# A fp32 decoder layer on one core: input blocks at the start, state-space chunks and the merge of the attention groups respread over the schedule

## The chip, the cores and the metric

The kernel runs on 1 core of one Trainium2 chip. The metric is the device time of one execution in microseconds (us): 888.43 us, the median of 3 runs (888.11 to 888.56). Engines are named as in the profile: PE (TensorE), DVE (VectorE), ACT (ScalarE), POOL (GpSimd) and SP (SyncE, which issues most DMAs here).

## What is computed

One layer, S = 512 tokens, D = 1024, all in fp32:

```python
proj = x @ w_in            # q, k, v (3 dilation groups x 8 heads x 64), u (512), gate logits (2 x 1024)
outs, lses = attention(q, k, v)          # per group: out and log of the softmax denominator
attn = sum(softmax(lses, over groups) * outs)
y_attn = attn @ w_attn_br
states = scan(a_bar, b_bar * u)          # 32 groups of 16 channels, complex 64-dim states
y = gelu(Re(C states) + D u)
a, b = split(y @ w_glu); y_ssm = (a * sigmoid(b)) @ w_ssm_br
h = layer_norm(ALPHA * x + (gates[0] * y_attn + gates[1] * y_ssm) @ w_out)
out = layer_norm(ALPHA * h + (silu(h @ w_ff_gate) * (h @ w_ff_up)) @ w_ff_down)
```

In the kernel dilation group 0 is attention "kind 0", groups 1 and 2 are taken together as "kind 1"; the merge weighs kind 0 against kind 1 by their maxima and denominators.

## The kernel before

**Products.** Each fp32 operand is split into a high part (rounded, by ACT, L178) and a low part (the rest, by DVE, L179); `mm3` (L184) makes hi·hi, lo·hi and hi·lo, the lines L185, L186, L187 of the profile. A product with 8 blocks of 128 rows is 24 matmuls of 128x512.

**Weights.** They come as 1 MB units (two weight tiles each) by a DMA of SP into one of two raw buffers. `Weights.split` (ACT `whi`, DVE `wlo`) fills one of three slots; `release` at the end of a step frees a slot, and so lets the tile three steps later be split. A weight tile's `wlo` therefore stands in DVE's queue behind whatever a step gave to DVE before its end.

**Steps.** PE runs through steps n: 0 to 3 make u (the state-space input), 4 to 7 v of group 0 (each with a transposition `tv` one step later), 8 to 19 gates, 20 to 27 k and q of group 0, 28 to 51 v, k, q of groups 1 and 2, 52 to 55 gates. Then 4 GLU tiles (56 to 59), 8 branch tiles BR0 to BR7 (60 to 67; 0 to 3 read the GLU's `gh`, `gl`, 4 to 7 the merged attention `ath`, `atl`), the output product, the feed-forward part. All other work is hung into the steps by `at_step(n, fn)`: at n it runs in the middle of the step's tile (or behind it, in the GLU tiles), at n + 0.5 at its end. Small DVE operations of the state-space model wait in a list `late`, from which `drip(first, last, cols)` takes about `cols` columns every half step.

**What the change touches.** At the start x comes in five DMAs and the first u unit in three, in turn (L249 to L263); the first two u tiles are made together (`u_first`), the other two as steps 2 and 3. `u_turn` sends u through DRAM, `make_pm` (step 6) transposes the matrices `zs`, `state_inputs` (steps 8 and 8.5) makes 64 small matmuls each, in banks that the transpositions use too (scores: banks 3, 4; turned: 5, 6), and ACT copies the four banks out. `ssm_out` (24.5, 25.5) makes y and its GELU on ACT and DVE in turn. At the end `split_y` (55) splits y for the GLU, `merge_stats` (56) turns the statistics of both kinds into 8 rows (`stb`, `sts`), then come `merge_weights` (57, with a reciprocal), `merge_split` (58, hi and lo rows in `whl`) and four `merge_pair` (59.5 to 62.5), in which two matmuls for each kind, one for the hi rows and one for the lo rows, spread the weights over 128 partitions (`wb`), and DVE makes the merged output.

Of the kernel before, what the change touches and what calls it, by code (L numbers as in the profile page):

```python
# [1329 lines left out]
```

## Time and profile before

| | before |
|---|---|
| time, median of 3 runs | 888.43 us (888.11 to 888.56) |
| the profiled execution | 889.8 us, of it a span of 887.9 us |
| mean granted clock of PE over the span | 0.993 |
| busy: PE, DVE, ACT | 868.0, 496.0, 292.9 us |

The span is what the profiler records from the first to the last instruction; 1.9 us of the profiled execution lie outside it. Times of the trace are us from the span's start. PE's matmuls are pipelined: the record of a 128x512 matmul is 0.39 us long, and the next one starts 0.227 us after it, so the step from one start to the next is the cost of one. A wait is the idle time in brackets behind a row of the timeline, with the work that ended it.

### The profile page before, as it was taken

The numbers are of one execution on the slowest core, as the hardware profiler recorded it, in microseconds if no ns is written. First come the engines' busy times: TensorE is split into PE (matmuls) and PEld (weight loads), VectorE is DVE, ScalarE is ACT, GpSimd is POOL, SyncE is SP. The second block draws the span as 40 slices with busy tenths as digits, with TensorE's granted clock in tenths as the row PEclk, the third lists the DMA queues.
The fourth block names the chain that finished last, engine by engine and source line by source line (L and its number), as shares of the span: only waits on it lengthen the run. The fifth ranks groups of instructions, "written<-read, shape, count | busy, mean of one in ns | idle before, by whom it ended". The sixth has DMA issues, their size and how long they took to land.

```text
span 887.9 us, 11787 instructions
## 1 busy us (share of the span) xinstructions
PE 868.0 (98%) x4822; PEld 716.7 (81%) x4822; DVE 496.0 (56%) x951; ACT 292.9 (33%) x478; POOL 25.1 (3%) x26
## 2 busy tenths in 40 slices
PE   8989999989999999998999999999999999999996
PEld 5878888878878888876788898888888888888885
DVE  7865999765365455347876764444444444222237
ACT  5354332344442234554234233222222222211111
POOL 0000000000000000000000410000000000000004
PEclk9999999999999999999999999999999999999998
DMA  8832423234212212112316313222222222422203
GB/s 307 184 101 97 102 71 102 89 96 143 89 54 96 85 59 96 48 50 75 108 55 245 134 55 137 94 95 95 96 94 96 95 95 94 142 95 95 94 1 96
DMA packets 23782, 90.04 MB, mean 101 GB/s; under 512 B 5672, under 2 KB 10792, under 8 KB 14512
## 3 DMA queue, kind: packets, MB, share of 16 engines
q1 hardware_dynamic: 22144, 86.80, 29.4%
q10 hardware_dynamic: 1584, 2.48, 0.8%
q8 instruction: 38, 0.62, 0.3%
q14 instruction: 16, 0.13, 0.0%
HBM read 84.85 MB, written 4.42 MB: 101 GB/s over the span
## 4 chain that ended last, share of the span: by engine, by line
PE 48%; issue 40%; DVE 7%; ACT 3%; POOL 2%; DMA 1%; SPq 0%; DVEq 0%; POOLq 0%
PE pg L185 3%; PE pg L187 3%; PE pg L186 3%; PE pv L186 3%; PE pv L187 3%; PE pv L185 3%; PE pk L185 3%; PE pk L187 2%; PE pk L186 2%; PE pq L185 2%; PE pq L187 2%; PE pq L186 2%; PE s L764 2%; PE t L788 2%; PE o L802 2%
## 5 line engine op out<-in xcount | busy, mean ns | idle before, releaser
L179 DVE TENSOR_TENSOR wlo<-raw,whi 128x1024 fp32r<-128x1024 f32 x136 | 166.3, 1227 | 205.5 <-ACT whi L178 205.4
L178 ACT CAST whi<-raw 128x1024 fp32r<-128x1024 f32 x136 | 141.6, 1046 | 205.6 <-PE dn L187 74.8
L185 PE MATMUL fg<-hh,whi 128*128 128x512 f32 (+1 forms) x384 | 143.5, 374 | 0.0
L187 PE MATMUL fg<-hh,wlo 128*128 128x512 f32 (+1 forms) x384 | 143.4, 373 | 0.0
L186 PE MATMUL fg<-hl,whi 128*128 128x512 f32 (+1 forms) x384 | 143.4, 373 | 0.0
L186 PEld LDWEIGHTS fg<-hl,whi 128*128 128x128 f32 x384 | 72.3, 188 | 13.3
L187 PEld LDWEIGHTS fg<-hh,wlo 128*128 128x128 f32 x384 | 72.3, 188 | 13.3
L185 PEld LDWEIGHTS fg<-hh,whi 128*128 128x128 f32 x384 | 72.3, 188 | 13.3
L185 PE MATMUL dn<-whi,ff 128*128 128x512 f32 x168 | 66.0, 393 | 0.0
L187 PE MATMUL dn<-whi,ff 128*128 128x512 f32 x168 | 65.9, 392 | 0.0
L186 PE MATMUL dn<-wlo,ff 128*128 128x512 f32 x168 | 65.8, 392 | 0.0
L185 PE MATMUL pg<-x_hi,whi 128*128 128x512 f32 x128 | 51.0, 399 | 0.0
L187 PE MATMUL pg<-x_hi,wlo 128*128 128x512 f32 x128 | 50.5, 395 | 0.0
L186 PE MATMUL pg<-x_lo,whi 128*128 128x512 f32 x128 | 50.5, 395 | 0.0
L181 ACT ACTIVATE ff<-fth 128x512 fp32r<-128x512 f32 x22 | 13.9, 634 | 101.6 <-DVE fth L301 101.6
L301 DVE TENSOR_TENSOR fth<-fth,fg 128x512 f32<-128x512 f32 x22 | 15.1, 688 | 55.8 <-PE fg L187 55.6
L776 ACT ACTIVATE pt<-pt,st 128x256 f32<-128x256 f32 (+1 forms) x64 | 30.9, 485 | 45.7 <-DVE st L774 45.7
L186 PE MATMUL pv<-wlo,x_hi 128*128 128x256 f32 x128 | 37.0, 289 | 2.7 <-DVE wlo L179 2.7
L185 PE MATMUL pq<-x_hi,whi 128*128 128x512 f32 x96 | 38.2, 398 | 0.0
L185 PE MATMUL pk<-x_hi,whi 128*128 128x512 f32 x96 | 37.8, 394 | 0.0
L186 PE MATMUL pq<-x_lo,whi 128*128 128x512 f32 x96 | 37.5, 390 | 0.0
L187 PE MATMUL pq<-x_hi,wlo 128*128 128x512 f32 x96 | 37.4, 390 | 0.0
(247 smaller groups left out, 1566.0 us busy)
## 6 DMA issues: line engine op xcount, KB each, us to landing
raw<-in_w_in SPq DMA_DIRECT2D x27, 1024.0 KB, 4.8
raw<-in_w_gu SPq DMA_DIRECT2D x22, 1024.0 KB, 4.8
raw<-in_w_dn SPq DMA_DIRECT2D x11, 1024.0 KB, 4.7
raw<-in_w_br SPq DMA_DIRECT2D x4, 1024.0 KB, 4.8
raw<-in_w_out SPq DMA_DIRECT2D x4, 1024.0 KB, 4.7
raw<-in_w_glu SPq DMA_DIRECT2D x2, 1024.0 KB, 4.8
xn<-in_x SPq DMA_DIRECT2D x2, 1024.0 KB, 8.2
out_dram<-hn SPq DMA_DIRECT2D x13, 128.0 KB, 2.4
```

The lines of the kernel that those rows point to most:

```text
L178: act.copy(hi, src)
L179: dve.tensor_tensor(lo, src, hi.bitcast(F32), op=ALU.subtract)
L181: act.mul(hi, src, scale)
L185: pe.matmul(dst, a[0], b[0], start=first, stop=False)
L186: pe.matmul(dst, a[0], b[1], start=False, stop=False)
L187: pe.matmul(dst, a[1], b[0], start=False, stop=last)
L301: eng.tensor_tensor(o, a, b, op=op)
L764: pe.matmul(banks[hh][:, 256 * j + 128 * c : 256 * j + 128 * (c + nk)], z[0][rows, hp, qs], z[1][rows, hp, 128 * k0 : 128 * (k0 + nk)], st ...
L776: act.activation(pt[:, :n], pt[:, :n], AF.Exp, bias=mneg, scale=-1.0, accum_out=zsum)
L788: pe.transpose(tb[:, hh, cs], pts[hh][:, cs], ident)
L802: pe.matmul(ob[64 * hh : 64 * hh + 64, 128 * blk : 128 * blk + 128], z[2][:, kb, 64 * h : 64 * h + 64], tv[:, hh, 128 * c : 128 * c + 128] ...
```

## The change

- **Start.** Both u units come in blocks of x's rows: x block 0, u block 0, x block 1, u block 1 and so on (256 KB each up to block 3, then pairs of 512 KB). `u_tiles` makes all four u tiles at once, in banks 3 to 6: for each block four hi·hi, four with x's low part, four with the weights' low part. The first split waits for no `late` operations ahead of it.
- **State inputs.** `state_inputs` goes in four parts, at 7, 7.5, 8 and 8.5, of 32 matmuls and two copies each.
- **Drips and the state-space output.** `late` is taken by 2000 columns (4 to 9), 1600 (9 to 20) and 500 (20 to 28) for 1900 (4 to 20) and 700 (20 to 24.5). `ssm_out` moves to 28 and 29 with its GELU in batches of two halves, `turn_y` to 30, the attention turns of kind 0 from 27 + 1.5 j to 30 + 1.5 j.
- **Merge.** The statistics of kind 0 are turned at step 52; everything from `split_y` to the reciprocal stands at 55.5, `merge_split` at 57, the pairs at 58 to 61. Hi and lo rows stand in one operand of 40 rows (8 hi, 24 zero, 8 lo), so that `wb` is one matmul for each kind; POOL clears the operand.
- **Loops.** In the GLU loop what hangs on n comes after the tile's weights are released; a branch tile runs its first three blocks for both columns, then block 3 of the first, what hangs on n, and block 3 of the second.

```diff
-TURNS = [[27 + 1.5 * j for j in range(10)], ...
+TURNS = [[30 + 1.5 * j for j in range(10)], ...
-    load_x(0, 1)
-    load_u(slice(0, 2))
-    load_x(1, 2)
-    load_u(slice(2, 4))
-    load_x(2, 4)
-    load_u(slice(4, 8))
-    load_x(4, 6)
-    load_x(6, 8)
-    w.n_dma = 1
-    w.n_split = 2
+    for k0, k1 in ((0, 1), (1, 2), (2, 3), (3, 4), (4, 6), (6, 8)):
+        load_x(k0, k1)
+        load_u(k0, k1)
+    w.n_dma = 2
+    w.n_split = 4
...
-    late.take(14)
-    split_x(0)
-    late.take(6)
-    split_u(slice(0, 2))
...
+    for k in range(KT):
         split_x(k)
+        split(wup[0][k // 4][:, k % 4], wup[1][k // 4][:, k % 4], wu[k // 4][:, k % 4])
+        late.take(4 if k < 2 else 10)
...
+    def u_tiles():
+        bs = [bank(3 + e, f"pu{e}") for e in range(4)]
         for k in range(KT):
+            xk = kslice(xp, k)
+            for a, b in ((0, 0), (0, 1), (1, 0)):
+                for e in range(4):
+                    wk = kslice(wup, k, slice(128 * e, 128 * e + 128))
+                    pe.matmul(bs[e], wk[a], xk[b], start=(k + a + b == 0), stop=(k == KT - 1 and a == 1))
+        for e in range(4):
             u_evac(bs[e], e)
...
-    def state_inputs(r):
+    def state_inputs(r, m):
...
-        for m in range(2):
-            bs = [(scores, turned)[m](f"sb{r}{m}{half}") for half in range(2)]
+        bs = [(scores, turned)[m](f"sb{r}{m}{half}") for half in range(2)]
...
-            act.square(y2, yf)
-            ts(y2, y2, 0.044715, ALU.mult, 1.0, ALU.add)
-            tt(y2, y2, yf, ALU.mult)
-            act.activation(y2, y2, AF.Tanh, scale=math.sqrt(2.0 / math.pi))
-            stt(yf, y2, 1.0, yf, ALU.add, ALU.mult)
+        for a, b in zip(y2, yf):
+            act.square(a, b)
+            ts(a, a, 0.044715, ALU.mult, 1.0, ALU.add)
+            tt(a, a, b, ALU.mult)
+        for a, b in zip(y2, yf):
+            act.activation(a, a, AF.Tanh, scale=math.sqrt(2.0 / math.pi))
+            stt(b, a, 1.0, b, ALU.add, ALU.mult)
...
     def merge_split():
...
+        act.copy(sel, rope[64:104, 0].rearrange("h (p m) -> h p m", p=NPAIR))
+        pool.memset(hl[0:40, 0:1024].bitcast(F32), 0.0)
+        for (m, _), w_ in zip(merged["s"], merged["w"]):
+            tt(m, m, merged["z"], ALU.mult)
+            act.copy(w_[0:8], m)
+            tt(w_[32:40], m, w_[0:8].bitcast(F32), ALU.subtract)
...
-            for e in range(2):
-                pe.matmul(wb[kind], merged["sel"][:, hp, :], merged["w"][kind][e], start=(e == 0), stop=(e == 1))
+            pe.matmul(wb[kind], merged["sel"][:, hp, :], merged["w"][kind], start=True, stop=True)
...
-    drip(4, 20, 1900)
-    drip(20, 24.5, 700)
+    drip(4, 9, 2000)
+    drip(9, 20, 1600)
+    drip(20, 28, 500)
...
-    at_step(8, state_inputs, 0)
-    at_step(8.5, state_inputs, 1)
+    for r in range(2):
+        for m in range(2):
+            at_step(7 + r + 0.5 * m, state_inputs, r, m)
...
-        at_step(24.5 + rnd, ssm_out, rnd)
-    at_step(26.5, turn_y)
+        at_step(28 + rnd, ssm_out, rnd)
+    at_step(30, turn_y)
...
-    at_step(55, split_y)
-    at_step(56, merge_stats)
-    at_step(57, merge_weights)
-    at_step(58, merge_split)
+    at_step(52, merge_stats, 0)
+    for fn in (split_y, lambda: merge_stats(1), merge_shift, merge_sum, merge_reciprocal):
+        at_step(55.5, fn)
+    at_step(57, merge_split)
     for hp in range(NPAIR):
-        at_step(59.5 + hp, merge_pair, hp)
+        at_step(58 + hp, merge_pair, hp)
...
-        run_fill(N_GLU + n)
         th = at.tile([P, 512], F32, tag="sw", name=f"th{n}")
...
         w.release()
+        run_fill(N_GLU + n)
...
+        part(0, range(3))
+        part(1, range(3))
+        part(0, (3,))
+        run_fill(N_BR + n)
+        part(1, (3,))
```

**Three places in the order of instructions.** First DVE around the first `ssm_out`; `ysb` is y, `y2` its GELU, the `rope` rows belong to a q tile, `wlo` is a weight tile's low part. Before:

```order
L298 SCALAR_TENSOR_TENSOR ysb_1512<-y2_00_1569,ysb_1512 128x512
L301 TENSOR_TENSOR ysb_1512<-ysb_1512,yc00_1515 128x2x128
L301 TENSOR_TENSOR ysb_1512<-ysb_1512,yc01_1516 128x2x128
L295 TENSOR_SCALAR y2_01_1579<-y2_01_1579 128x512
L301 TENSOR_TENSOR y2_01_1579<-y2_01_1579,ysb_1512 128x512
L298 SCALAR_TENSOR_TENSOR ysb_1512<-y2_01_1579,ysb_1512 128x512
L714 STREAM_SHUFFLE swq01_1610<-pq01_1585 128x512
L301 TENSOR_TENSOR cqq01_1611<-pq01_1585,rope_105 128x512
L301 TENSOR_TENSOR swq01_1610<-swq01_1610,rope_105 128x512
L301 TENSOR_TENSOR q0_1474<-cqq01_1611,swq01_1610 128x4x128
L179 TENSOR_TENSOR wlo1_28_1617<-raw14_1437,whi1_28_1616 128x1024
```

and now:

```order
L297 TENSOR_TENSOR q0_1473<-cqq03_1609,swq03_1608 128x4x128
L179 TENSOR_TENSOR wlo2_30_1615<-raw15_1509,whi2_30_1614 128x1024
L297 TENSOR_TENSOR ysb_1644<-ysb_1644,yc00_1647 128x2x128
L297 TENSOR_TENSOR ysb_1644<-ysb_1644,yc01_1648 128x2x128
L297 TENSOR_TENSOR ysb_1644<-ysb_1644,yc00_1647 128x2x128
L297 TENSOR_TENSOR ysb_1644<-ysb_1644,yc01_1648 128x2x128
L291 TENSOR_SCALAR y2_00_1697<-y2_00_1697 128x512
L297 TENSOR_TENSOR y2_00_1697<-y2_00_1697,ysb_1644 128x512
L291 TENSOR_SCALAR y2_01_1698<-y2_01_1698 128x512
L297 TENSOR_TENSOR y2_01_1698<-y2_01_1698,ysb_1644 128x512
L294 SCALAR_TENSOR_TENSOR ysb_1644<-y2_00_1697,ysb_1644 128x512
L294 SCALAR_TENSOR_TENSOR ysb_1644<-y2_01_1698,ysb_1644 128x512
```

Before, the ten operations of the first `ssm_out` (the last six are shown) stand between two q tiles and ahead of the low part of the tile of step 28, `wlo1_28`. Now they stand behind `wlo2_30`, in steps 28 and 29, which have no rope; the ten of the second follow them directly, and then `wlo0_31`, the tile of step 31.

Second ACT from step 7 to step 9; `sb` are the banks of the state inputs, `sst` what they are copied into, `tv` the transposed v, `vt` v before it, `whi` a weight tile. Before:

```order
L733 COPY v0_436<-tv02_626 128x4x128
L726 COPY vt3_644<-pv03_606 128x4x128
L178 CAST whi1_10_646<-raw5_472 128x1024
L593 COPY sst0_680<-sb000_681 128x4x16x8
L593 COPY sst0_680<-sb001_682 128x4x16x8
L593 COPY sst0_680<-sb010_701 128x4x16x8
L593 COPY sst0_680<-sb011_702 128x4x16x8
L733 COPY v0_436<-tv03_721 128x4x128
L877 ACTIVATE gt0_658<-pg0_659,bgate_107 128x512
L178 CAST whi2_11_740<-raw5_472 128x1024
L593 COPY sst1_748<-sb100_749 128x4x16x8
L593 COPY sst1_748<-sb101_750 128x4x16x8
```

and now:

```order
L178 CAST whi2_9_594<-raw4_270 128x1024
L574 COPY sst0_628<-sb000_629 128x4x16x8
L574 COPY sst0_628<-sb001_630 128x4x16x8
L716 COPY v0_435<-tv02_649 128x4x128
L709 COPY vt3_667<-pv03_607 128x4x128
L178 CAST whi0_10_669<-raw5_471 128x1024
L574 COPY sst0_628<-sb010_682 128x4x16x8
L574 COPY sst0_628<-sb011_683 128x4x16x8
L574 COPY sst1_722<-sb100_723 128x4x16x8
L574 COPY sst1_722<-sb101_724 128x4x16x8
L716 COPY v0_435<-tv03_743 128x4x128
L864 ACTIVATE gt0_702<-pg0_703,bgate_116 128x512
```

The copies `sst` come in pairs, one pair ahead of the copy of `tv02` and two ahead of that of `tv03`, where all four of the first state input stood ahead of `tv03`.

Third DVE in the merge, from the sum of the denominators on; `sts` and `rope` hold the rows of both kinds, `th` and `gl` belong to the GLU tiles, `wlo` is a weight tile, `whl` the operand of the spreading matmuls. Before:

```order
L301 TENSOR_TENSOR zg_3710<-sts_3633 8x512
L840 RECIPROCAL zg_3710<-zg_3710 8x512
L298 SCALAR_TENSOR_TENSOR th1_3715<-th1_3715,gl10_3684 128x512
L182 SCALAR_TENSOR_TENSOR gl_3604<-th1_3715,gh_3603 128x512
L179 TENSOR_TENSOR wlo0_60_3721<-raw30_3494,whi0_60_3720 128x1024
L846 CAST selr_3750<-sel_3631 8x512
L301 TENSOR_TENSOR sts_3633<-sts_3633,zg_3710 8x512 x2
L301 TENSOR_TENSOR whl_3752<-sts_3633,whl_3752 8x512 x2
L298 SCALAR_TENSOR_TENSOR th2_3761<-th2_3761,gl20_3724 128x512
L182 SCALAR_TENSOR_TENSOR gl_3604<-th2_3761,gh_3603 128x512
L179 TENSOR_TENSOR wlo1_61_3767<-raw30_3494,whi1_61_3766 128x1024
```

and now:

```order
L297 TENSOR_TENSOR sts_3615<-rope_114,sts_3615 8x512
L831 RECIPROCAL sts_3615<-sts_3615 8x512
L294 SCALAR_TENSOR_TENSOR th0_3665<-th0_3665,gl00_3639 128x512
L182 SCALAR_TENSOR_TENSOR gl_3638<-th0_3665,gh_3637 128x512
L179 TENSOR_TENSOR wlo1_59_3671<-raw29_3354,whi1_59_3670 128x1024
L294 SCALAR_TENSOR_TENSOR th1_3711<-th1_3711,gl10_3685 128x512
L182 SCALAR_TENSOR_TENSOR gl_3638<-th1_3711,gh_3637 128x512
L179 TENSOR_TENSOR wlo2_60_3717<-raw30_3506,whi2_60_3716 128x1024
L297 TENSOR_TENSOR rope_114<-rope_114,sts_3615 8x512
L297 TENSOR_TENSOR whl_3721<-rope_114,whl_3721 8x512
L297 TENSOR_TENSOR sts_3615<-sts_3615 8x512
L297 TENSOR_TENSOR whl_3721<-sts_3615,whl_3721 8x512
```

The reciprocal stands ahead of the first GLU tile's operations, not behind them, and `whl` behind those of the second; kind 0's rows are finished before kind 1's are begun.

## Rows read from the trace of the kernel before

**Rows 1.** The first page: the line of the engines (busy time, share of the span, instructions).

```profile
PE 868.0 (98%) x4822; PEld 716.7 (81%) x4822; DVE 496.0 (56%) x951; ACT 292.9 (33%) x478; POOL 25.1 (3%) x26
```

**Rows 2.** The waits of PE: line and tile that waited, the releaser, the total in us, the times, the longest.

```profile
PE pv L186 <- DVE wlo L179: 2.7, 1, 2.7
PE tv L732 <- ACT sst L593: 2.1, 1, 2.1
...
PE b L185 <- ACT gh L181: 1.2, 1, 1.2
PE pu L186 <- DVE x_lo L179: 1.2, 2, 1.0
```

**Rows 3.** Four stretches in the view by windows: the window and its length, busy us and instructions of PE, PEld, DVE, ACT and POOL, the granted clock as a share of the full one, the DMA share and GB/s moved.

```profile
10.00:20.00 10.00, 9.01 (x37) 6.97 (x38) 9.69 (x48) 5.58 (x10) 0.00 (x0) 1.00 1.04 408
60.00:70.00 10.00, 7.95 (x117) 6.31 (x110) 3.58 (x15) 6.13 (x8) 0.00 (x0) 0.83 0.01 2
180.00:190.00 10.00, 7.32 (x38) 6.62 (x39) 8.70 (x21) 4.77 (x12) 0.00 (x0) 0.83 0.19 49
405.00:425.00 20.00, 17.72 (x72) 12.74 (x71) 16.48 (x19) 7.42 (x11) 0.00 (x0) 1.00 0.27 102
```

**Rows 4.** The timeline of ACT at the start: start, length, line, operation, tiles, shape, count, and in brackets the idle time before and what ended it.

```profile
3.65 0.62 ACT L178 CAST x_hi<-x_raw 128x512 fp32r<-128x512 f32 x1 [0.97 <-DMA x_raw<-in_xT]
...
5.35 0.71 ACT L178 CAST whi<-wu_raw 128x256 fp32r<-128x256 f32 x2 [1.08 <-DMA wu_raw<-in_w_in]
...
7.05 0.62 ACT L178 CAST x_hi<-x_raw 128x512 fp32r<-128x512 f32 x1 [0.99 <-DMA x_raw<-in_xT]
...
15.73 1.05 ACT L178 CAST whi<-raw 128x1024 fp32r<-128x1024 f32 x1 [1.35 <-DMA raw<-in_w_in]
```

**Rows 5.** The timeline of PE: the first product of the kernel, the first two of step 4, and the start of `make_pm`.

```profile
5.80 0.50 PE L185 MATMUL pu<-x_hi,whi 128*128 128x512 f32 x1 [0.46 <-ACT whi L178]
...
30.68 0.39 PE L185 MATMUL pv<-x_hi,whi 128*128 128x512 f32 x1
30.90 0.39 PE L186 MATMUL pv<-x_lo,whi 128*128 128x512 f32 x1
...
44.75 1.91 PE L513 MATMUL pt<-ident,zs 128*128 128x128 f32 x16
```

**Rows 6.** The timeline of DVE ahead of `make_pm`: the last of the `zs` operations that it transposes.

```profile
43.99 0.69 DVE L76 TENSOR_TENSOR zs<-zs,zd 128x512 f32<-128x512 f32 x1
```

**Rows 7.** The timeline of PE in step 8 and at the start of step 9, and of ACT between: the state inputs `sb`, their copies, and the products `pg` around them.

```profile
58.98 1.98 PE L590 MATMUL sb<-ut,pmT 64*64 64x128 f32 x64
...
63.01 0.66 PE L732 MATMUL tv<-ident,vt 128*128 128x128 f32 x4 [2.05 <-ACT sst L593]
...
65.00 0.63 PE L186 MATMUL pg<-x_lo,whi 128*128 128x512 f32 x1
65.42 0.63 PE L187 MATMUL pg<-x_hi,wlo 128*128 128x512 f32 x1
...
69.85 0.50 PE L185 MATMUL pg<-x_hi,whi 128*128 128x512 f32 x1
...
60.11 3.75 ACT L593 COPY sst<-sb 128x512 f32<-128x512 f32 x4 [1.74 <-PE sb L590]
```

**Rows 8.** The timeline of PE in step 28 (two rows running behind the long wait), and of DVE at the end of `ssm_out`, where step 28's tile waits, and earlier, in step 24.

```profile
187.13 0.58 PE L186 MATMUL pv<-wlo,x_hi 128*128 128x256 f32 x1 [2.68 <-DVE wlo L179]
...
188.57 0.41 PE L186 MATMUL pv<-wlo,x_hi 128*128 128x256 f32 x1
188.78 0.41 PE L187 MATMUL pv<-whi,x_lo 128*128 128x256 f32 x1
...
182.39 0.69 DVE L298 SCALAR_TENSOR_TENSOR ysb<-y,ysb 128x512 f32<-128x512 f32 x1 [0.70 <-ACT y L692]
...
185.85 1.22 DVE L179 TENSOR_TENSOR wlo<-raw,whi 128x1024 fp32r<-128x1024 f32 x1
...
156.79 1.22 DVE L179 TENSOR_TENSOR wlo<-raw,whi 128x1024 fp32r<-128x1024 f32 x1
```

**Rows 9.** The timeline of ACT in step 52: the copies of the attention turn.

```profile
358.09 1.05 ACT L790 COPY tv<-t 128x512 f32<-128x512 f32 x2
```

**Rows 10.** The timeline of PE from the end of step 55 to the fourth branch tile: the attention values behind step 55, the first transposes of the merge, the products `wb` that spread its weights, and the first of branch tile 4.

```profile
386.21 1.09 PE L802 MATMUL o<-tv,v 128*64 128x128 f32 x16
...
393.74 1.04 PE L821 MATMUL stb<-ident,st 128*8 128x128 f32 x8
...
409.55 0.50 PE L185 MATMUL gl<-yh,whi 128*128 128x512 f32 x1 [0.82 <-DVE th L298]
...
415.34 1.19 PE L863 MATMUL wb<-whl,selr 8*128 8x512 f32 x4
...
444.42 0.40 PE L185 MATMUL b<-ath,whi 128*128 128x512 f32 x1
```

**Rows 11.** The timeline of DVE in the merge: the reciprocal, a GLU tile's last operation with a weight tile behind it, and the two low parts of the weights `whl`.

```profile
405.61 3.34 DVE L840 RECIPROCAL zg<-zg 8x512 f32<-8x512 f32 x1
...
410.19 0.69 DVE L182 SCALAR_TENSOR_TENSOR gl<-th,gh 128x512 fp32r<-128x512 f32 x1 [0.70 <-ACT gh L181]
...
411.13 1.23 DVE L179 TENSOR_TENSOR wlo<-raw,whi 128x1024 fp32r<-128x1024 f32 x1 [0.25 <-ACT whi L178]
...
413.96 1.29 DVE L301 TENSOR_TENSOR whl<-sts,whl 8x512 fp32r<-8x512 f32 x2
```

More of the change, by code (lines that the diff above doesn't have):

```diff
@@ L45 @@
 NLAST = 4
-TURNS = [[27 + 1.5 * j for j in range(10)], [46, 47.5, 49, 50, 51.5, 52.5, 53.5, 54.5, 55.5, 56.5]]
+TURNS = [[30 + 1.5 * j for j in range(10)], [46, 47.5, 49, 50, 51.5, 52.5, 53.5, 54.5, 55.5, 56.5]]
 TOKENS = np.arange(S).reshape(128, 4).T.reshape(-1)
@@ L681, in ssm_out @@
                                       start=(r == 0), stop=(r == 1))
+        is_ = slice(2 * rnd, 2 * rnd + 2)
+        yf = [y[:, half, is_].rearrange("p i b c -> p (i b c)") for half in range(2)]
+        y2 = [at.tile([P, 512], F32, tag="sw", name=f"y2_{rnd}{half}") for half in range(2)]
         for half in range(2):
-            is_ = slice(2 * rnd, 2 * rnd + 2)
             for par in range(2):
@@ L834, in merge_weights, with merge_stats @@
[L834 to L857 removed]
+    def merge_stats(kind):
+        if kind == 0:
+            merged["s"] = [[rope[0:8, e, :] for e in range(2)]]
+            sp.dma_start(rope[64:104, 0], i["sel"].rearrange("h p m -> h (p m)"))
+        else:
+            z = big(1, "sts")
+            merged["s"].append([z[0:8, 512 * e : 512 * (e + 1)] for e in range(2)])
+            merged["raw"] = z
+        for e in range(2):
+            b = turned(f"stb{kind}{e}")
+            for blk in range(4):
+                pe.transpose(b[0:8, 128 * blk : 128 * blk + 128], st[kind][:, e, blk, :], ident)
+            if kind == 0:
+                dve.tensor_copy(by_phase(merged["s"][0][e]), as_phases(b[0:8]))
+            else:
+                dve.tensor_copy(merged["s"][1][e], b[0:8])
@@ new lines, in merge_shift, with merge_sum @@
+    def merge_shift():
+        (m0, _), (m1, _) = merged["s"]
+        mg = merged["raw"][0:8, 1024:1536]
+        tt(mg, m0, m1, ALU.min)
+        for m in (m0, m1):
+            tt(m, mg, m, ALU.subtract)
+        for m in (m0, m1):
+            act.activation(m, m, AF.Exp)
+    def merge_sum():
+        (m0, z0), (m1, z1) = merged["s"]
+        merged["z"] = zg = merged["raw"][0:8, 1536:2048]
+        tt(z0, m0, z0, ALU.mult)
+        tt(z1, m1, z1, ALU.mult)
+        tt(zg, z0, z1, ALU.add)
@@ new lines, in merge_reciprocal @@
+    def merge_reciprocal():
+        dve.reciprocal(merged["z"], merged["z"])
+    def merge_split():
+        sel = at.tile([40, NPAIR, P], F32R, tag="tv", name="selr")
+        hl = big(0, "whl", F32R)
+        merged.update(sel=sel, w=[hl[0:40, 512 * k : 512 * (k + 1)] for k in range(2)])
+        act.copy(sel, rope[64:104, 0].rearrange("h (p m) -> h p m", p=NPAIR))
[4 more added lines that the diff above has]
+            tt(w_[32:40], m, w_[0:8].bitcast(F32), ALU.subtract)
@@ L941, in emit @@
                 at_step(n, attn_turn, kind, *pairs[j - 1])
[L942 to L945 removed]
+    at_step(52, merge_stats, 0)
+    for fn in (split_y, lambda: merge_stats(1), merge_shift, merge_sum, merge_reciprocal):
+        at_step(55.5, fn)
+    at_step(57, merge_split)
     for hp in range(NPAIR):
[L947 to L955 removed]
+        at_step(58 + hp, merge_pair, hp)
+    for _ in range(3):
+        w.split()
+        late.take(12)
+    u_tiles()
+    run_fill(3.5)
+    for n in range(4, N_GLU):
         kind, g, un, c = STEPS[n]
@@ L1281, in layout @@
     gu = np.stack([a["w_ff_gate"][0].reshape(D, NFF, P), a["w_ff_up"][0].reshape(D, NFF, P)], 2).reshape(D, 2 * DFF)
-    parts = [units(p, 8, 256) if j in (6, 9) else pairs(p, 8, P) for j, p in enumerate(parts)]
+    parts = [units(p, 4, 512) if j == 0 else units(p, 8, 256) if j in (6, 9) else pairs(p, 8, P) for j, p in enumerate(parts)]
     def state(m):
```

132 lines of the change are left out of this document (28 added, 104 removed).

## The prediction

> **What bounds the kernel now.** I read the list of engines first, then the waits of PE, then the windows around each wait, and last the timelines of the engine that is waited for. PE is busy for 868.0 of 887.9 us, DVE for 496.0, ACT for 292.9 [rows 1]: only what PE waits for, what it does with a slower clock, and how many instructions it has can move the time. The waits are few, and four of them hold most of the sum [rows 2]: 2.7 us for a weight tile's low part in step 28, 2.1 for the copies of the state inputs, 1.2 for `gh` in the first branch tile, 1.2 for low parts of x at the start. Two of them cost more than their length. In the windows 60:70 and 180:190 the granted clock is 0.83, elsewhere 1.00 [rows 3]: behind the wait of 2.05 us PE starts matmuls 0.42 us apart [rows 7], behind that of 2.68 us 256-column ones 0.21 apart [rows 8], where at full clock a 512-column one takes 0.227 (from 30.68 to 44.75 [rows 5] stand 60 of them and one transposition of 0.45: 13.6 / 60). That is the level of 1.2 GHz in place of 2.4. Through 405:425 the clock stays 1.00, though waits of 0.82 and 1.24 lie in it [rows 2, 3, 10]. So a wait of over 2 us costs itself and the slow matmuls behind it.
>
> **Start.** The 96 matmuls of the four u tiles stay. Before, they run from 5.80 to 30.68 [rows 5], 24.9 us, of which 96 x 0.227 = 21.8 is work and 3.1 is waits and restarts. Now each block of x gives PE 12 matmuls, 2.72 us, while DVE needs two low parts of 128x512 for it (0.69 each, the shape of the row in [rows 6]) and up to ten small operations, together under 2.5. The first block is whole when the second 256 KB have come; they were at ACT at 5.35 [rows 4], so PE starts at about 6.0. 6.0 + 21.8 + 0.3 for the restart gives 28.1, a gain of 2.6. Behind it come steps 4, 5 and half of 6, and `make_pm` before started at 44.75 [rows 5], right behind the last `zs` operation, which ended at 44.7 [rows 6]. With PE 2.6 earlier DVE must be as early. Its small operations lose the cover of the first wait for data, but it has idled between tiles; I put the last `zs` at 42.0 to 42.5 and PE at 42.1. **2.5** gained, 1.5 to 2.9.
>
> Four of the pieces are of 512 KB and eight of 256 KB, where the weight units are 1 MB. In the window 10:20 the pieces, one behind the other, moved 408 GB/s [rows 3], and the raw unit behind all 4 MB was at ACT at 15.73 [rows 4]. At that rate each block is there before PE wants it, and the sum goes by that. The Trainium skill, DMA: Bandwidth & Descriptors, section Bandwidth, speaks against the change: it asks for transfers of at least 1 MiB to reach three quarters of the peak. The traffic of 10:20 does not agree with it for queued pieces; the first three do (rival 4).
>
> **State inputs.** Before, step 8 loses 2.05 us of wait (the 64 matmuls use four banks, and the transposition `tv` needs one that ACT has not copied out: four copies take 3.75 [rows 7]) and then nine matmuls at 0.42 or 0.43 for 0.227, 1.8 us. Now two copies (1.9) follow each 32 matmuls. The transposition of step 8 comes half a step (2.7) and 32 matmuls (1.0) behind the previous part, 3.7 us; ACT has in this time 0.6 for v, 1.04 for `whi` and one copy to do before the bank is free, 2.8. Step 8.5 leaves about the same 0.7. So no wait, and no slow clock; 0.1 goes for two more breaks in the stream. **3.8** gained of 3.85; 3.0 if one of the two margins is missed by a little.
>
> **State-space output.** Before, DVE works at `ssm_out` with waits of 0.70 on ACT [rows 8] between q tiles, so that `wlo` of step 28 starts at 185.85 and PE waits 2.68. Behind it 14 matmuls run at 0.21 for 0.12 (half the 512-column step, rounded up), 1.3 us, and 0.2 is lost at the restart: 4.2. Moved to 28 and 29, the operations stand where no rope is to be done. From the middle of step 29 PE has 24 x 0.12 + 24 x 0.227 = 8.3 us before it wants the tile of step 31; DVE's ten operations (six of 0.69, four of half the width), a wait of 0.7 and the `wlo` of 1.2 take about 7.4. In steps 20 to 27 the drip now costs DVE an operation each half step; a rope and a `wlo` there leave a tile of 5.44 us slack (the `wlo` at 156.79 [rows 8] starts over a step ahead of its use). **4.2** gained, 2.5 to 4.4. `turn_y` and the attention turns move by three steps with the same work; I cost them at nothing, covered by the dense stream of PE, and up to 0.4 either way if one more bank is late.
>
> **Merge.** I walk it from the end of step 55, at 386.21 [rows 10], as t = 0; BR4 began at t = 58.2. At 52 there are 8 transposes more (1.04, the row at 393.74 [rows 10]) and a wait of about 1.1 for the attention copies of ACT, which end at 359.1 [rows 9]: 2.1 lost. Behind 55: the attention values and transposes to 1.9, 0.5 wait for their copies, 8 transposes, 0.4 wait for y's first part, the GLU tile of 24 matmuls in 5.6 (before: from 388.1, 1.9 behind 386.21, to 393.74 [rows 10]); the last values; GLU1 from 10.6 to 16.2, GLU2 to 21.8. Then `wb` of kind 0. DVE's chain up to it: reciprocal from 11.3 to 14.6 (3.34 [rows 11]); `th0`, `gl`, `wlo` and `th1`, `gl`, `wlo`, each with 0.7 and 0.25 of waits on ACT, to 21.3; then product, ACT's cast and low part for kind 0 to 23.3 and for kind 1 to 25.3 (0.65 each on DVE, 0.6 on ACT). So PE waits 1.6, does one matmul, and waits 1.75. GLU3 starts at 25.6 (before 23.3), BR0 at 31.8 without the waits of 1.24 and 0.22; one wait of 0.95 in BR0 for the merged rows; BR1 at 38.8; BR4 at 55.8. The eight `wb` matmuls saved are 2.2 of that (a group of four is 1.19 long with its pipelined end [rows 10], about 1.12 without). So 2.4 better here, 2.1 worse at 52: **+0.3** at full clock. The two waits, with one matmul between them, are together longer than either that lowered the clock, and I take it that it falls here too: 9 matmuls at 0.2 more, or 14 at 0.09, is 1.3 to 1.8. **1.2** lost; bounds 3 lost (both waits a us longer) to 2 gained (DVE 1.7 earlier).
>
> **Sum.** 2.5 + 3.8 + 4.2 - 1.2 = 9.3. The profiled execution took 889.8 and would take 880.5; what stands around the span is the same, so 888.43 gives **879.1**.
>
> **Rivals.** (1) No fall of the clock at `wb`, or shorter waits there: 877.6, and with the best of each bound 875. For it: 0.25 us of work between the two waits, and waits of 0.82 and 1.24 left the clock alone. (2) DVE lags: the drip of 500 per half step over steps 20 to 27, or `ssm_out` ahead of `wlo0_31`, brings the wait of 2.7 with its slow matmuls back, 4.2: 883.3. For it: a margin of 1 us at step 31; against: no rope there. (3) The state inputs only move their wait: the margins of 0.7 fail in both places, a us each and then 0.2 for a restart, and `zs` keeps `make_pm` at 43.5: 3.5 less, 882.6. (4) The first blocks set the pace: 256 KB came 1.70 apart (3.65, 5.35, 7.05 [rows 4]). If all 4 MB came so, the last block would be there at 3.65 + 15 x 1.70 = 29.2, the u tiles would end at 33, 2.3 later than before, and the time is 883.9. Against it stand the 408 GB/s and the 15.73. This is what the Trainium skill's rule on 1 MiB (the page named above) would make of the start. (5) Slower: the clock falls at `wb` and stays low. A 512-column matmul then costs 0.2 more. The three other steps and the merge at full clock gain 10.8, so 54 slow matmuls take all back; GLU3, BR0 and BR1 at that level (72) cost 14.4, and the time is 892.0. For it: further waits follow (0.95 in BR0); against: the low stretches of before ended after 9 and 14 matmuls [rows 3, 7, 8].
>
> **How the numbers follow.** Forecast 0.44, rival 1 0.22, rival 2 0.12, rival 3 0.10, rival 4 0.07, rival 5 0.05. About 0.2%, 1.8 us, is what a measurement can tell from no change; two of the rivals 2 to 4 together give 887 or so, and 0.03 of their chance is "same". Faster 0.92, same 0.04, slower 0.04. The range goes from 875.0 (rival 1 with DVE earlier) to 884.5 (rival 4, rounded up) and leaves out the pairs of rivals, rival 5 and luck beyond the bounds, under 0.2.
>
> **What would show it.** Start: step 4's first product near 28.1, no wait of PE in 6 to 28, `make_pm` near 42.3. State inputs: no wait for `sst`, the clock 1.00 between 55 and 70. Output: no wait for `wlo` between 140 and 200, clock 1.00. Merge: waits for `whl` at the first `wb` pair, 1.6 and 1.75, with a low clock in GLU3; none for `gh` in BR0. A wait over 1 us that stands in none of these places, or a clock below 1.00 there, would make the sum wrong.

## The result, and the profile after

| | before | changed |
|---|---|---|
| time, median | 888.49 us (4 runs, 888.11 to 890.05) | 882.16 us (4 runs, 881.04 to 883.05) |
| ratio, 95% interval | | 0.9925 [0.9907, 0.9942] |
| span of the profiled execution | 887.9 us | 881.3 us |

The change is worth 6.3 us; 9.3 were forecast, which is beyond the interval of the measurement (5.2 to 8.3 us), and 882.16 lies between the 875.0 and 884.5 that were given. Where the 3 us went is read by laying the two timelines of PE side by side and noting how much earlier the same instruction starts. The columns of all timelines are those of the rows ahead of the prediction.

| PE reaches | before | after | earlier by | of it in this part | forecast |
|---|---|---|---|---|---|
| step 4, first product | 30.68 | 28.30 | 2.38 | start 2.4 | 2.5 |
| `make_pm` | 44.75 | 42.37 | 2.38 | | |
| the 128 matmuls of step 11 (`kb`) | 83.67 | 78.39 | 5.28 | state inputs 2.9 | 3.8 |
| last v product | 337.50 | 327.82 | 9.68 | state-space output 4.4 | 4.2 |
| last transposes of attention | 387.23 | 379.65 | 7.58 | merge, step 52: -2.1 | -2.1 |
| BR4, first product | 444.42 | 437.69 | 6.73 | merge, behind 55: -0.9 | +0.9 |

The rows of the kernel before that this table uses beside those of [rows 5, 10]:

```profile
83.67 1.98 PE L528 MATMUL kb<-ca,bb 64*16 64x64 f32 x128
...
337.50 0.28 PE L187 MATMUL pv<-whi,x_lo 128*128 128x256 f32 x1
...
387.23 1.09 PE L788 MATMUL t<-ident,pt 128*128 128x128 f32 x8
```

and those of the kernel after, with the first product and the statistics of step 52:

```profile
5.68 1.92 PE L548 MATMUL pu<-x_hi,wuh 128*128 128x512 f32 x4 [0.35 <-ACT wuh L178]
...
28.30 0.39 PE L185 MATMUL pv<-x_hi,whi 128*128 128x512 f32 x1
...
42.37 1.91 PE L493 MATMUL pt<-ident,zs 128*128 128x128 f32 x16
...
78.39 1.98 PE L508 MATMUL kb<-ca,bb 64*16 64x64 f32 x128
...
327.82 0.28 PE L187 MATMUL pv<-whi,x_lo 128*128 128x256 f32 x1
...
349.03 1.08 PE L808 MATMUL stb<-ident,st 128*8 128x128 f32 x8 [0.97 <-ACT tv L773]
...
379.65 1.09 PE L771 MATMUL t<-ident,pt 128*128 128x128 f32 x8
```

The view of PE's waits of the kernel after (line, releaser, total, times, longest) answers to [rows 2]:

```profile
PE wb L850 <- DVE whl L297: 3.3, 2, 1.7
...
PE stb L808 <- ACT tv L773: 1.3, 2, 1.0
PE wb L850 <- DVE a L297: 0.4, 1, 0.4
```

The waits for `wlo`, for `sst`, for `gh` and for `th` are gone. In the merge there are now two for `whl`, two for `tv` ahead of the statistics (one of them in step 52) and one of 0.4 for an operation of a pair. Windows of the kernel after, for [rows 3]:

```profile
60.00:70.00 10.00, 10.00 (x80) 7.94 (x73) 2.71 (x9) 6.00 (x7) 0.00 (x0) 1.00 0.26 86
180.00:190.00 10.00, 10.00 (x148) 9.28 (x147) 5.26 (x11) 4.62 (x11) 0.00 (x0) 1.00 0.01 2
400.00:410.00 10.00, 6.75 (x16) 4.54 (x16) 7.49 (x10) 3.31 (x6) 0.00 (x0) 0.66 0.18 58
```

The two stretches at 0.83 are at full clock and PE is busy throughout; 400:410 has fallen to 0.66 and PE works for 6.75 of 10 us. The timeline of PE there, and BR4, which answer to [rows 10]:

```profile
402.04 0.50 PE L850 MATMUL wb<-whl,selr 40*128 40x512 f32 x1 [1.58 <-DVE whl L297]
404.20 0.76 PE L850 MATMUL wb<-whl,selr 40*128 40x512 f32 x1 [1.67 <-DVE whl L297]
404.89 0.79 PE L185 MATMUL gl<-yh,whi 128*128 128x512 f32 x1
...
409.33 0.63 PE L186 MATMUL gl<-ych,whi 128*128 128x512 f32 x1
...
410.14 0.40 PE L185 MATMUL gl<-yh,whi 128*128 128x512 f32 x1
...
412.99 0.73 PE L850 MATMUL wb<-whl,selr 40*128 40x512 f32 x2
...
437.69 0.40 PE L185 MATMUL b<-ath,whi 128*128 128x512 f32 x1
```

Both waits for `whl` stand where the walk had put them, and are 1.58 and 1.67 long for 1.6 and 1.75. Then the clock is low from the second `wb` matmul to 410.1, and the 24 matmuls of GLU tile 3 take 8.1 us (404.89 to 412.99) where a GLU tile at full clock takes 5.6.

PE around the state inputs, for [rows 7]:

```profile
55.08 1.10 PE L572 MATMUL sb<-ut,pmT 64*64 64x128 f32 x32
56.12 0.50 PE L185 MATMUL pg<-x_hi,whi 128*128 128x512 f32 x1
...
59.10 1.10 PE L572 MATMUL sb<-ut,pmT 64*64 64x128 f32 x32
...
60.14 0.66 PE L715 MATMUL tv<-ident,vt 128*128 128x128 f32 x4
...
63.49 1.10 PE L572 MATMUL sb<-ut,pmT 64*64 64x128 f32 x32
64.52 0.50 PE L185 MATMUL pg<-x_hi,whi 128*128 128x512 f32 x1
```

No row has a wait. But the twelve products from 56.12 to 59.10 take 2.98 where 12 x 0.227 is 2.72: the three stretches of twelve between two breaks lose 0.22 to 0.26 each. Before, the twelve ahead of the first `sb` (56.16 to 58.98) took 2.82 and lost 0.10.

### The profile page after: what moved, and what is told of

Same layout as the page of the kernel before. It is cut to its first block, busy times and chain, and to the rows that moved or that the text cites. A ratio compares the mean times of both kernels' runs of the same rounds, so it can differ in the third digit from the quotient of the medians.

```text
span 881.3 us, 11787 instructions
## 1 busy us (share of the span) xinstructions
PE 865.2 (98%) x4814; PEld 715.7 (81%) x4814; DVE 496.4 (56%) x950; ACT 294.3 (33%) x479; POOL 26.0 (3%) x27
## 4 chain that ended last, share of the span: by engine, by line
PE 45%; issue 41%; DVE 8%; ACT 3%; POOL 2%; DMA 1%; SPq 0%; DVEq 0%; POOLq 0%; ACTq 0%
PE pg L185 3%; PE pg L186 3%; PE pg L187 3%; PE pv L185 3%; PE pu L548 3%; PE pv L187 3%; PE pv L186 3%; PE pk L185 3%; PE pq L185 3%; PE pq L187 2%; PE pk L187 2%; PE pq L186 2%; PE pk L186 2%; PE s L747 2%; DVE wlo L179 2%
## 5 line engine op out<-in xcount | busy, mean ns | idle before, releaser
L179 DVE TENSOR_TENSOR wlo<-raw,whi 128x1024 fp32r<-128x1024 f32 x134 | 164.1, 1228 | 203.4 <-ACT whi L178 203.2
L178 ACT CAST whi<-raw 128x1024 fp32r<-128x1024 f32 x134 | 139.6, 1046 | 217.5 <-PE dn L187 74.8
L187 PEld LDWEIGHTS dn<-whi,ff 128*128 128x128 f32 x168 | 31.5, 188 | 7.3
L187 PE MATMUL pk<-x_hi,wlo 128*128 128x512 f32 x96 | 37.4, 390 | 0.0
L186 PE MATMUL pk<-x_lo,whi 128*128 128x512 f32 x96 | 37.4, 390 | 0.0
```

What stands on the lines that cost most here:

```text
L178: act.copy(hi, src)
L179: dve.tensor_tensor(lo, src, hi.bitcast(F32), op=ALU.subtract)
L186: pe.matmul(dst, a[0], b[1], start=False, stop=False)
L187: pe.matmul(dst, a[1], b[0], start=False, stop=last)
```

## The experiments

Twelve kernels ran. Each is compared with the kernel before on the same chip; since the runs of that kernel scatter by up to 4.5 us (the last section shows what goes with it), versions of the change are set against each other by their own medians and by their timelines. Three chips were used, one for e1 to e4, one for e5 to e8, one for e9 to e12; the kernel before has medians of 889.12, 888.51 and 889.08 us on them, so differences of under a us between versions of different groups are not told from the chips'.

| version | median, us | range | ratio to before, interval |
|---|---|---|---|
| the change | 882.16 | 881.04 to 883.05 | 0.9925 [0.9907, 0.9942] |
| e1_old_merge | 879.25 | 879.17 to 880.56 | 0.9887 [0.9868, 0.9906] |
| e2_pairs_late | 876.92 | 876.55 to 877.17 | 0.9857 [0.9839, 0.9875] |
| e3_fill | 880.12 | 879.66 to 881.49 | 0.9896 [0.9877, 0.9915] |
| e4_scores | 880.25 | 880.01 to 881.41 | 0.9897 [0.9879, 0.9916] |
| e5_old_state | 880.27 | 879.18 to 882.11 | 0.9906 [0.9891, 0.9920] |
| e6_old_ssm_time | 877.12 | 876.97 to 877.49 | 0.9871 [0.9857, 0.9884] |
| e7_old_start | 879.93 | 879.68 to 881.86 | 0.9907 [0.9892, 0.9922] |
| e8_banks | 876.12 | 875.95 to 876.51 | 0.9860 [0.9846, 0.9873] |
| e9_old_gelu_old_time | 881.29 | 879.93 to 883.61 | 0.9915 [0.9897, 0.9933] |
| e10_old_gelu | 879.98 | 878.50 to 880.26 | 0.9894 [0.9879, 0.9910] |
| e11_best | 875.46 | 875.12 to 875.50 | 0.9846 [0.9831, 0.9860] |
| e12_before_gelu | 884.64 | 883.42 to 886.44 | 0.9952 [0.9936, 0.9967] |

**e1: the old merge.** The functions of the merge, its steps, the GLU loop and the branch loop are those of before.

```diff
...
-    at_step(52, merge_stats, 0)
-    for fn in (split_y, lambda: merge_stats(1), merge_shift, merge_sum, merge_reciprocal):
-        at_step(55.5, fn)
-    at_step(57, merge_split)
+    at_step(55, split_y)
+    at_step(56, merge_stats)
+    at_step(57, merge_weights)
+    at_step(58, merge_split)
     for hp in range(NPAIR):
-        at_step(58 + hp, merge_pair, hp)
+        at_step(59.5 + hp, merge_pair, hp)
```

> The changed kernel with the merge, the GLU loop and the branch loop of the kernel before; start, state inputs and state-space output stay changed. Theory (the merge as changed costs about 2.9 us, the other three parts give 9.7 together): 878.8 us, PE's waits at th 0.8 and gh 1.2 return, granted clock 1.00 in 400:410. Rival (the saved spreading matmuls and waits pay for the new waits, and the missing 3 us lie outside the merge): 882 or more.

879.25: the new merge costs 2.9 us, as the two timelines said, and the other three parts are worth 9.2 (by the medians) to 9.7 (by the table above). The waits at `th` and `gh` are back with 1.09 and 1.35, and the clock in 400:410 is 1.00. The rival falls.

**e2: the pairs one tile later.**

```diff
-        at_step(58 + hp, merge_pair, hp)
+        at_step(59 + hp, merge_pair, hp)
```

> The four pairs stand one GLU or branch tile later (59 to 62 for 58 to 61), so that GLU tile 3 runs while DVE finishes whl. Theory (the two waits for whl cost 3.3 and the slow clock behind them 2.5, and nothing takes their place): no wait for whl, clock 1.00 through the merge, 876.3 us. Rival (the wait moves on to gh, th or the merged rows in the branch tiles, and brings the slow clock with it): 879 to 882 with waits of over 1 us in 60 to 64.

876.92, 5.2 less than the change. No wait for `whl` is left. A part of the rival came too: the second pair waits 1.28 for a bank that DVE still reads, which is the 0.6 that the time is above the forecast, and more.

```profile
412.25 0.70 PE L850 MATMUL wb<-whl,selr 40*128 40x512 f32 x2 [1.28 <-DVE a L297]
```

**e3: work in the place of the wait.** The output of the added matmuls is not used.

```diff
+        if hp == 0:
+            fb = outs("fillb")
+            for _ in range(14):
+                pe.matmul(fb, w.views[N_GLU + 3][0][:, 0, 0:128], gluin["y"][0][:, 0, :], start=True, stop=True)
```

> 14 matmuls of 128x512 whose output nobody reads run ahead of the first wb matmul, on operands that are ready there, so that PE is busy while whl is made; no wait is shortened by it. Theory (the clock falls because PE idles, and the fall costs 2.5 us beyond the wait): the waits before wb shrink to under 1 us together, GLU tile 3 starts at the same time as before (within 0.4), runs its 24 matmuls in 5.6 instead of 8.1, and the time falls by 2 to 2.5 to about 880. Rival (the slow matmuls come from something else, such as a read of the 40-row operand or DVE beside it): GLU tile 3 stays at 8.1 us and the time stays at 882 or rises.

880.12 with 3.2 us more work, and the clock of the whole span at 0.996 to 0.998 in all four runs (0.994 to 0.996 in the change). The timeline of PE in this kernel:

```profile
400.17 3.34 PE L851 MATMUL fillb<-yh,whi 128*128 128x512 f32 x14
403.43 1.07 PE L854 MATMUL wb<-whl,selr 40*128 40x512 f32 x2
404.44 0.50 PE L185 MATMUL gl<-yh,whi 128*128 128x512 f32 x1
...
410.10 0.73 PE L854 MATMUL wb<-whl,selr 40*128 40x512 f32 x2
```

GLU tile 3 starts at 404.44 (404.89 in the change) and takes 5.66 us for 8.10. That separates the two prices: 3.3 us of waits and 2.4 of slow clock behind them, and in this place it is the idling of PE that the clock answered to, since all else is as it was. The profiled run is the slowest of the four (881.49): behind the merge it has a wait of 0.92 for `hn` by POOL, which no other profile here has.

**e4: other banks for the statistics.**

```diff
-            b = turned(f"stb{kind}{e}")
+            b = scores(f"stb{kind}{e}")
```

> The turned statistics of both kinds go into the banks of the scores (3, 4) instead of those of the turned probabilities (5, 6). Theory (the wait of 0.97 at step 52 is for a bank that ACT has not copied out yet): that wait and the 0.27 at 55.5 vanish, 1.1 to 1.3 less, 881.0 us. Rival (another wait stands right behind it: the scores of the next turn then wait for DVE's copies of the statistics): the wait comes back as s or stb by DVE, and the time stays at 882.

Both waits for ACT's `tv` are gone, so it was the bank. Between the last q product (341.26, in the change 341.78) and the last transposes (377.95, 379.65) PE wins 1.18 us; 0.44 of wait stands behind it now, for `yh` in GLU tile 0. In the profiled execution the clock fell for a shorter time (0.83 in 400:410), so that the whole 1.9 of the median is not the bank's.

The next versions but e11 and e12 have the later pairs of e2, with which the clock stayed at 0.997 in all four runs, so 876.92 is what they are set against.

**e5: the old state inputs.**

```diff
...
-    for r in range(2):
-        for m in range(2):
-            at_step(7 + r + 0.5 * m, state_inputs, r, m)
+    at_step(8, state_inputs, 0)
+    at_step(8.5, state_inputs, 1)
```

> The kernel with the pairs one tile later (876.9 us), with the state inputs as before the change: 64 matmuls at 8 and 64 at 8.5. Theory (splitting them saves a wait of 2 us and nine slow matmuls, 3.85, and gives 0.9 back in breaks of the dense stream): 879.9 us, the wait for sst of about 2 and a granted clock of 0.83 return between 50 and 70. Rival (the part of the 5.3 us won by step 9 that I put down to the state inputs comes from the earlier start): under 1 us slower, 877 to 878.

880.27, 3.35 more; the wait for `sst` is back, and the clock in 60:70 is 0.83.

```profile
60.33 0.68 PE L717 MATMUL tv<-ident,vt 128*128 128x128 f32 x4 [2.04 <-ACT sst L576]
```

The matmuls of step 11 start at 80.99 instead of 77.83, 3.2 later; 0.3 of it is there before the state inputs begin (the first transposition behind `make_pm` stands at 44.35 for 44.06), so that 2.9 is theirs, as in the table.

**e6: the old places of the state-space output.** Drips, `ssm_out`, `turn_y` and the attention turns of kind 0 are where they were; the GELU stays in batches of two.

```diff
-TURNS = [[30 + 1.5 * j for j in range(10)], ...
+TURNS = [[27 + 1.5 * j for j in range(10)], ...
-    drip(4, 9, 2000)
-    drip(9, 20, 1600)
-    drip(20, 28, 500)
+    drip(4, 20, 1900)
+    drip(20, 24.5, 700)
-        at_step(28 + rnd, ssm_out, rnd)
-    at_step(30, turn_y)
+        at_step(24.5 + rnd, ssm_out, rnd)
+    at_step(26.5, turn_y)
```

> The kernel with the pairs one tile later (876.9 us), with the drips, the state-space output, turn_y and the turns of attention kind 0 at their old steps (24.5, 25.5, 26.5, 27 + 1.5 j); the GELU stays in batches. Theory (the new places alone remove the wait for the low part of step 28 and the slow matmuls behind it): 881 to 882 us, or more since PE reaches step 24.5 5.3 us earlier than before while DVE has no less to do; a wait for wlo between 160 and 190 and a clock under 1.00 behind it. Rival (the batched GELU, with half the waits of DVE on ACT, is what removes it): 877 to 878, no wait over 1 us there.

877.12. My theory falls: at the old places the wait does not come back. DVE's timeline shows why (the first `ssm_out` and the weight tile behind the next rope):

```profile
157.31 1.41 DVE L297 TENSOR_TENSOR ysb<-ysb,yc 128x256 f32<-128x256 f32 x4
158.75 0.43 DVE L291 TENSOR_SCALAR y<-y 128x512 f32<-128x512 f32 x1
...
160.88 1.48 DVE L294 SCALAR_TENSOR_TENSOR ysb<-y,ysb 128x512 f32<-128x512 f32 x2
...
165.13 1.21 DVE L179 TENSOR_TENSOR wlo<-raw,whi 128x1024 fp32r<-128x1024 f32 x1
```

No row has a wait: while ACT squares one half, DVE works on the other. In the old order DVE waited 0.70 for ACT at each square and each tanh ([rows 8] has one of these rows), eight times in the two outputs, 5.6 us, where 2.7 made the tile late. The next three runs take the two halves of this part of the change apart.

**e9: old places and old GELU.** The diff of e6 and that of e10 below: the GELU of each half runs in one go as before.

> The kernel with the pairs one tile later (876.9 us), with the state-space output, drips, turn_y and turns of attention kind 0 at their old steps and the GELU in its old order as well. Theory now (the batched GELU alone takes the wait of step 28 away: in the old order DVE waits eight times 0.70 us for ACT, 5.6 us, more than the 2.7 that the tile was late): the wait for the low part of step 28 is back, 2.5 to 3, with slow matmuls behind it, about 881 us. Rival (the earlier start and state inputs shifted DVE's work so far that the old order fits too): 877 us, no wait for wlo.

881.29, 4.2 more than e6 by the medians and 2.9 by the profiled runs (879.93 and 877.02, both at a clock of 0.997), with only the order of the GELU between them. The wait of step 28 is back with 2.65. In the profiled execution, the fastest of the four (879.93), no slow matmul follows it:

```profile
181.08 0.39 PE L186 MATMUL pv<-wlo,x_hi 128*128 128x256 f32 x1 [2.65 <-DVE wlo L179]
181.30 0.28 PE L187 MATMUL pv<-whi,x_lo 128*128 128x256 f32 x1
181.42 0.28 PE L185 MATMUL pv<-whi,x_hi 128*128 128x256 f32 x1
```

**e10: new places and old GELU.**

```diff
...
-        for a, b in zip(y2, yf):
-            act.square(a, b)
...
-        for a, b in zip(y2, yf):
-            act.activation(a, a, AF.Tanh, scale=math.sqrt(2.0 / math.pi))
-            stt(b, a, 1.0, b, ALU.add, ALU.mult)
+            act.square(y2, yf)
...
+            act.activation(y2, y2, AF.Tanh, scale=math.sqrt(2.0 / math.pi))
+            stt(yf, y2, 1.0, yf, ALU.add, ALU.mult)
```

> The kernel with the pairs one tile later (876.9 us), with the GELU in its old order, at the new steps 28 and 29. Theory (either half of the change would do in steps 20 to 28, but in the old order the second output ends some 2 us later and the tile of step 31, whose low part has little to spare, comes late): a wait for wlo of 0.5 to 2 us at step 31, 877.5 to 879.5 us. Rival (the new place alone is enough): no wait for wlo, 876.9 us.

879.98, half a us above the forecast range. The wait for `wlo` stands at step 31:

```profile
195.16 0.50 PE L187 MATMUL pk<-x_hi,wlo 128*128 128x512 f32 x1 [0.53 <-DVE wlo L179]
```

By the last v product PE is 1.22 later than in e2 (328.47, 327.25), nearly all of it lost behind step 11 (77.91, 77.83). That much is the order's. The rest of the 3.1 is a fall of the clock in the merge, which e2 does not have behind the same wait of 1.28 (last section); the one run of e10 whose clock is 0.997 like e2's took 878.50, 1.6 more.

**e12: the batched GELU alone, in the kernel before.** The diff of the change in `ssm_out`, nothing else.

> The kernel before with nothing changed but the order of the GELU in the state-space output (both halves' squares and products first, then both tanh). Theory (the eight waits of DVE on ACT are what makes step 28's tile late): the wait of 2.68 and the low clock in 180:190 go, 4.0 to 4.4 less, 884.2 us. Rival (DVE is behind by the sum of its work in 24 to 28, whatever the order): the wait shrinks by under 1 us and the time stays over 887.

884.64, ratio 0.9952 [0.9936, 0.9967], 4.4 less than before on that chip (2.9 to 5.7 by the interval). The wait for `wlo` is gone from the view of waits, and the window that stood at 0.83 in [rows 3] reads:

```profile
180.00:190.00 10.00, 10.00 (x72) 8.99 (x72) 6.64 (x17) 3.39 (x10) 0.00 (x0) 1.00 0.68 181
```

So of the third part of the change the order of ten operations is worth the whole gain, within the noise. The new steps by themselves are worth a part: with the old order they shorten the wait from 2.65 to 0.53, and e10 is 1.3 faster than e9 by the medians and 1.7 by the last v product (328.47, 330.19). The two gains do not add up, since there is one wait to be won.

**e7: the old start.** Loads, splits and u tiles as before, steps 0 to 3 in the loop.

```diff
...
-    for _ in range(3):
-        w.split()
-        late.take(12)
-    u_tiles()
-    run_fill(3.5)
-    for n in range(4, N_GLU):
+    late.take(2)
+    w.split()
+    u_first()
+    late.take(20)
+    w.release()
+    w.release()
+    for n in range(2, N_GLU):
```

> The kernel with the pairs one tile later (876.9 us), with the start as before: u weights in one unit by three DMAs, two u tiles together, then two steps. Theory (the start is worth 2.4 us and is handed through to the end, since DVE keeps up): 879.3 us, step 4's first product at 30.7. Rival (the later steps have slack that swallows it, a wait in steps 4 to 9 being shorter when PE comes later): 877 to 878.

879.93, 3.0 more; step 4 starts at 30.63 for 27.74 in e2, 2.89 later, and 2.88 of it are left at the last transposes of attention (381.95, 379.08). The gain is handed through whole up to there, and the time agrees.

**e8: more banks for the spread weights.** As e2 with e4, and:

```diff
-        wb = [turned(f"wb{hp}{k}") for k in range(2)]
+        wb = [(turned, scores)[hp % 2](f"wb{hp}{k}") for k in range(2)]
```

> The kernel with the pairs one tile later (876.9 us), the turned statistics in the banks of the scores, and the spreading products of the second and fourth pair in the banks of the scores too. Theory (the 1.28 us wait of the second pair is for a bank that DVE still reads, the 0.97 at step 52 for one that ACT has not copied): both vanish with their restarts, 2.3 to 2.6 less, 874.4 us. Rival (behind the bank stands the merged row itself: DVE's chain for the second pair is late anyway and PE waits at the next pair or in branch tile 4): 875.5 to 876.

876.12, just above the rival's time, by another way than it said. The wait of 1.28 is gone, and in branch tile 1 PE waits for the same operation of DVE:

```profile
414.86 0.47 PE L185 MATMUL b<-gh,whi 128*128 128x512 f32 x1 [1.36 <-DVE a L297]
```

The ring of the branch tiles is banks 0 to 3, and bank 3 is one of the scores': the branch tile now waits for the bank that the pair has taken. That it is bank 3 is read from the rings in the code; no run moved that bank alone.

**e11: the statistics in the scores' banks, the pairs at the old steps.**

```diff
-            b = turned(f"stb{kind}{e}")
+            b = scores(f"stb{kind}{e}")
-        at_step(58 + hp, merge_pair, hp)
+        at_step(59.5 + hp, merge_pair, hp)
```

> The turned statistics in the banks of the scores and the pairs at the old steps 59.5 to 62.5, the rest as changed. Theory (at 60.5 the second pair stands behind branch tile 0's gates, when DVE has finished the first, so the wait of 1.28 goes and the 1.4 of the version with more banks does not come): 874.4 us, no wait over 0.5 us between GLU tile 1 and the feed-forward part. Rival (DVE has too much to do in branch tiles 0 to 2, wherever the pairs stand: the wait goes to gh, gl or a bank of the branch tiles): 875.5 to 876.5.

875.46, ratio 0.9846 [0.9831, 0.9860], the fastest version of the study, 6.7 below the change. It is 1.1 above the forecast and at the rival's time: the second pair still waits for DVE, half as long, and 0.44 for `yh` remains.

```profile
411.43 0.70 PE L850 MATMUL wb<-whl,selr 40*128 40x512 f32 x2 [0.62 <-DVE a L297]
```

## Why the prediction was right, and where not

The sign, the range and the place of each gain and of the loss were right; the sum was 3 us too good, in two terms, and one term was right for a wrong reason. The time alone would have pointed elsewhere: 882.16 is nearest to the 882.6 of rival 3, of which nothing came.

- **Start, 2.4 for 2.5.** Step 4 began at 28.30 for 28.1, no wait of PE lay between 6 and 28 except inside the first four matmuls (about 0.85), and `make_pm` at 42.37 waited for nothing. e7 puts it at 3.0. The ten other profiled kernels with the new start reach step 4 at 27.28 to 28.20, the three with the old one at 30.63 to 30.68, so the change's own profile shows the least gain of all; what sets the start back in one run and not in another is open. Rival 4, blocks 1.70 us apart throughout, is out: the last of the twelve pieces was at ACT at 15.64, where before the same 4 MB took until 15.73, and all u tiles were done at 28.3. The prediction's 408 GB/s of 10:20 are not of the small pieces alone, and the same window of the kernel after (410) is not either. In 5:10, mostly pieces of 256 KB, that kernel moved 316 GB/s, in 10:15, mostly pieces of 512 KB, 398, in 15:20, mostly units of 1 MB, 423. The Trainium skill's rule on large transfers (DMA: Bandwidth & Descriptors, section Bandwidth) did not bear on the start: for the queued pieces of 512 KB the trace does not agree with it, since they moved 94% of what the larger units moved, and for those of 256 KB it leaves open whether their size or the start of the queue held them to 316.
- **State inputs, 2.9 for 3.8.** The mechanism holds: no wait, no low clock, and both come back in e5. The term mis-sized is "0.1 goes for two more breaks in the stream". Two more breaks cost 0.8: the four stretches of products between 45.03 and 63.49, 60 products, lose 0.93 to the breaks around them, some 0.6 more than the ones in their place before, and the four groups of small matmuls take 4.1 where the two took 3.9. That is 0.8 of the 0.9 that is missing, 0.4 for each break more.
- **State-space output, 4.4 for 4.2.** The sum was right, the step behind it not: "Moved to 28 and 29, the operations stand where no rope is to be done". I had read the waits of 0.70 in [rows 8] and the batching in the diff, and gave the batching no price. e6 gives 0.2, no more than the noise, for the places if the GELU is batched, e9 against e6 4.2 for the batching at the old places, e12 4.4 for it alone. That 4.2 came so near is luck: the reason given, the places alone, is worth 1.3 to 1.7 (e10 against e9) and leaves a wait. The margin that I had feared at step 31 is real: in e10, without the batching, it is overdrawn by 0.53.
- **Merge, -2.9 for -1.2.** At 52 the forecast 2.1 were lost, 0.97 of them a wait for the bank (e4). Behind 55 the waits at `wb` came at their places with their lengths. The term mis-sized is the clock's: "9 matmuls at 0.2 more, or 14 at 0.09, is 1.3 to 1.8". Here 12 products of GLU tile 3, the first with 0.37 more, cost 2.5, and the second `wb`, slow as well, 0.4 more, 2.9 for the 1.5 that the sum used; e3 took 2.4 of it away by keeping PE busy. The rest of the 1.8 that separates +0.9 from -0.9 is the second wait, which ended some 0.2 later than walked, and from BR0 to BR4 the walk fits (24.0 us). The matmuls saved are worth 1.8 and not the 2.2 of the prediction: a pair's group takes 0.66 to the next matmul's start for 1.12 before; no run changed them by themselves. The places for the pairs were the costly choice: one tile later, e2 is 5.2 faster with the same saving of eight matmuls.
- **Rival 5**, the clock staying low, did not come: 12 products, near the number of before. (The timelines of before have 8 and 13 slow matmuls where the prediction counts 9 and 14; their sums, 1.8 and 1.3, hold.) **Rivals 2 and 3** did not come either. **Rival 1** is what e2 and e3 show when the wait is not there. The sentence "So a wait of over 2 us costs itself and the slow matmuls behind it" does not hold as a rule: in e9 one of 2.65 was followed by no slow matmul, in e10 one of 1.28 was (last section).

## What to carry to other kernels

Where two engines pass one tile back and forth, look first for a second tile to put between, before moving the work elsewhere: ten reordered operations were worth 4.4 us by themselves, more than the move of the whole block by three steps (1.3 to 1.7). A wait of the busiest engine can have two prices, its length and what the clock then does; one more tile of lead for the chain, whose result was not needed sooner, was worth 5 us here. And each cut more of a dense stream by a run of small matmuls has a price of its own (0.4 us here), so spreading a block over more places must buy more than that.
